# A decoder layer on one core: the input and its first block of weights laid side by side in memory, in six transfers

## The chip, the cores and the metric

The kernel runs on one core of one Trainium2 chip, as a single launch. The metric is device time in microseconds (us). TensorE (PE) multiplies matrices, VectorE (DVE) and ScalarE (ACT) work element by element, GpSimd (POOL) and SyncE (SP) mostly start transfers, and 16 DMA engines carry them between the chip's memory (DRAM) and the core's own buffers of 128 partitions.

## The reference

One decoder layer over 256 tokens of 1024 features. The input is normalised, multiplied by one wide matrix, passed through four mixers of four heads each, multiplied by an output matrix, normalised, and added to the input:

```
h = rmsnorm(x, pre_norm_g)                      # x: 256 x 1024
proj = h @ w_in                                 # w_in: 1024 x 4104
p_gdn, p_hgrn, p_moba, p_diff = split(proj)     # 1032, 1024, 1024, 1024 columns
y = concat([gdn_branch(p_gdn), hgrn2_branch(p_hgrn), moba_branch(p_moba), diff_branch(p_diff)])
x = x + rmsnorm(y @ w_out, post_norm_g)         # w_out: 1024 x 1024
```

The first mixer (gated delta rule) takes q, k, v from the first 768 columns through a short convolution, forms a 64x64 lower triangular system for each chunk of 64 tokens and head, solves it, and runs a recurrence over the chunks. The second is a gated linear recurrence, the third and the fourth are softmax attentions. Each mixer has a gate of its own.

## The kernel before

**The products.** The host cuts w_in into eight blocks of columns (`W_BLOCKS`): gkq (q and k of the first mixer, 512 wide), gv (its v and gates, 520 wide), mqk and mvz (third mixer), dqk and dvz (fourth), hqf and hiz (second). A block is used in four pieces of 256 rows (two slices k of 128). Each product must hold more precision than one pass gives, so every weight piece `raw` is split into a rounded part `whi` (a copy on ACT) and the rest `wlo` (a subtraction on DVE), and x transposed is split in the same way into `hT_hi` (ACT) and `hT_lo` (DVE). TensorE then adds three products, hi by hi, lo by hi and hi by lo: 24 matmuls of 128x256 to a piece, 96 to a block. There are six `raw` buffers (here raw_96, 99, 102, 105, 111, 112) and four each of `whi` and `wlo`, so a later piece is loaded when an earlier one has been split, and is split when TensorE is through with an earlier one.

**The start.** ACT's queue brings the per-column constants and the first slice of x transposed (`pxt`) into a buffer tagged h_kd. SP's queue brings the rest: gkq in four transfers of 256 KB and two of 512 KB, between them the other seven slices of x (four transfers into buffers tagged prob), then gv in four pieces, with `xs` (x itself, for the norm) after the first, then the constants `cs` and `pr`, then the other weights. A row of such a transfer is 1 to 2 KB long per partition for x, 2 to 4 KB for the weights. The norm's factor is worked out from `xs` beside the products and multiplied in afterwards (`rs`, then `rrow`); the first that needs it on DVE is `t2k<-pj,rrow`.

**The middle.** From there DVE runs the convolution, the triangular systems and their inversion (`g_nb`, `g_y`, `g_d`), whose last two steps are `g_ya` and its transposition `g_xa`. TensorE needs g_xa for `gA<-g_xa,g_ee`, where the first mixer's recurrence starts. Between them DVE also writes the `wlo` of the blocks that TensorE multiplies meanwhile (mqk, dqk, mvz, then hqf). Of a block, the products with wlo may come later than those with whi.

**The order.** No scheduler of the compiler sets it. Every operation is recorded by `record` with a cost, and `Core.plan` simulates the engines with these costs and always takes the ready operation with the highest rank: the longest path to the end, plus `boost` (where the code marks a load or a split as urgent), plus `LEAD` for the part of the kernel it belongs to. `HOLD`, `SWITCH` and `STAY` say how dearly the planner takes a change of ACT's table and of TensorE's tile shape. `emit` (line 392, so nearly every row of the trace has L392; L405 in the changed kernel) then issues the operations in that order. So new costs and new leads move operations on every engine.

Of the kernel before, what the change touches and what calls it, by code (L numbers as in the profile page):

```python
# [16 lines left out]
try:  # L17
# [21 lines left out]
C_DQ, C_DK, C_DV, C_DZ = 3080, 3336, 3592, 3848  # L39


W_BLOCKS = (("gkq", C_GQ, 512), ("gv", C_GV, 520), ("hqf", C_HQ, 512), ("hiz", C_HI, 512),
            ("mqk", C_MQ, 512), ("dqk", C_DQ, 512), ("mvz", C_MV, 512), ("dvz", C_DV, 512))


K_TRI, K_AFT, K_BLK, K_BM, K_I16 = 0, 128, 256, 288, 292
# [45 lines left out]


class Op:
    __slots__ = ("eng", "fn", "args", "kw", "cost", "need", "preds", "succs", "rank", "left", "at", "order", "boost", "groups", "work", "part", "lat", "mode")


class Core:
# [2 lines left out]

    SETS = {AF.Exp: 6, AF.Ln: 6, AF.Silu: 18}
    OUT = ("out", "accum_out", "dst")
    HOLD = 34479
    SWITCH, KEEP, STAY = 95, 1e9, 8733
    LEAD = {'h': 7522, 'g': 6523, 'o': -111940, 'M': 5144, 'x': 39478, 'm': 28417, 'd': 3696, 'D': 2624}
    WINDOW = 4096 / 1.2
    LAT = {"PE": 200, "DVE": 170, "ACT": 170, "POOL": 170, "SP": 2600}

    def __init__(self, ctx, tc):  # L110
        self.tc, self.nc = tc, tc.nc
        nc = tc.nc
# [5 lines left out]
        self.boost, self.part = 0.0, "x"  # L118
        self.phys, self.turn, self.masks = {}, {}, {}
        self.sbuf, self.psum = {}, {}  # L120

# [50 lines left out]
    def record(self, eng, fn, cost, writes, reads, args, kw, need=None):  # L172
        op = Op()
        op.eng, op.fn, op.args, op.kw, op.cost, op.need = eng, fn, args, kw, cost, need
        op.preds, op.succs, op.boost, op.groups, op.work = set(), [], self.boost, (0, 1, 2, 3), 0.0
        op.part, op.lat, op.mode = self.part, self.LAT[eng], (128, 128)
        me = len(self.ops)
        for w, aps in ((False, reads), (True, writes)):
            for ap in aps:
                name = ap.tensor.name  # L180
                if name in self.psum:

                    b = self.psum[name]
# [40 lines left out]
    def mm(self, out, lhsT, rhs, start=True, stop=True, **kw):  # L224
        n, m = self.size(rhs), lhsT.shape[1]
        full = 1.667 if rhs.dtype == F else .417
        cost = max(n * full, m * full) + 2 if rhs.dtype == F else max(n * .446, 107) + 4.5
        self.record("PE", "matmul", cost, [out], [lhsT, rhs], (out,),
                    dict(lhsT=lhsT, rhs=rhs, start=start, stop=stop, **kw))
        p, m = self.rows(out)  # L230
        o = self.ops[-1]
        if 2 < m < 128:
            o.groups = tuple(range(p // 32, (p + m + 31) // 32))
        k = self.rows(rhs)[1]
# [60 lines left out]
    def plan(self, noise=None):  # L295
# [22 lines left out]
        cols, mode, work = [0.0] * 4, (128, 128), {}  # L318
        while events:
            t = events[0][0]  # L320
            while events and events[0][0] <= t:
# [3 lines left out]
            for e, q in ready.items():  # L325
# [32 lines left out]
                if e == "PE":  # L358
# [9 lines left out]
                    end = o.at + cost * slow  # L368
                    for g in o.groups:
                        cols[g] = end  # L370
                    free[e] = end if len(o.groups) == 4 else o.at + 7 * slow
                heapq.heappush(events, (free[e], 1, -1))
                for s in o.succs:
                    n = ops[s]
# [17 lines left out]
            getattr(self.engines[o.eng], o.fn)(*o.args, **o.kw)  # L392


def build(tc, x, pxt, w_in, w_out, cst, prow, out, dbg=None):
    with ExitStack() as ctx:
        _build(Core(ctx, tc), x, pxt, w_in, w_out, cst, prow, out, dbg)


def bc(ap, n):  # L400
# [2 lines left out]
    return ap.unsqueeze(len(s)).to_broadcast(s + [n])  # L403


def _build(c, x, pxt, w_in, w_out, cst, prow, out, dbg):
# [6 lines left out]
    px = c.tile("px", [128, 512], tag="h_kd")  # L413
    pc = c.tile("pc", [128, P_END])
    pr = c.tile("pr", [128, R_POST])

    xr = [c.tile("xr", [128, 2, T], tag=f"prob_{i}") for i in range(4)]
# [22 lines left out]

    def piece(key, k):

        if (key, k) not in HI:
            t = c.tmp("raw", [128, 2, 520], bufs=6)
            w, o = BLOCKS[key], BLOCK_AT[key] + k * 128 * BLOCKS[key]
            part = bass.AP(tensor=w_in.tensor, offset=w_in.offset + o, ap=[[2 * w, 128], [w, 2], [1, w]])
            lead = sum(1 for q in HI if q[0] != "o")
            first = lead < 4
            if first:
                for i in range(2):  # L450
                    c.boost = turn(k + i) - 0.05 * BOOST
                    c.dma(t[:, i, :w], part[:, i])
            else:
                c.boost = turn(k) - 0.05 * BOOST if lead < 8 else turn(8) if lead < 10 else 0.0
                c.dma(t[:, :, :w], part)
            split([(key, k), (key, k + 1)], t[:, :, :w], first, not lead)
        return HI[key, k], LO[key, k]

    def split(keys, raw, apart=False, first=False):

        w = raw.shape[2]
        c.boost = BOOST
        hi = c.tmp("whi", [128, 2, 520], bufs=4, dt=FR)[:, :, :w]
        lo = c.tmp("wlo", [128, 2, 520], bufs=4, dt=FR)[:, :, :w]
        for i in ([slice(0, 1), slice(1, 2)] if apart else [slice(0, 2)]):
            if first and i.start == 0:
                c.copy(hi[:, i], raw[:, i])
            else:
                act(hi[:, i], raw[:, i], AF.Copy)
            c.tt(lo[:, i], raw[:, i], hi[:, i].bitcast(F), OP.subtract)  # L470
# [24 lines left out]
    for k in range(8):  # L495
        c.boost = BOOST + 500.0
        g = px[:, P_PRE + k:P_PRE + k + 1]
        xk = xr[k // 2][:, k % 2] if k else px[:, P_END:P_END + T]
# [729 lines left out]
def _arrays(inputs):  # L1228
# [9 lines left out]
    xt = a["x"].reshape(T, 8, 128).transpose(2, 1, 0).reshape(128, 8 * T)  # L1238
    blocks = [a["w_in"][0][:, c0:c0 + w].reshape(4, 2, 128, w).transpose(0, 2, 1, 3).reshape(-1) for _, c0, w in W_BLOCKS]
    return {"x": a["x"].reshape(T, D), "pxt": np.ascontiguousarray(np.concatenate([pcol, xt], axis=1)),  # L1240
            "w_in": np.concatenate(blocks)[None], "w_out": a["w_out"][0], "cst": _shape_constants(),
            "prow": np.ascontiguousarray(prow)}


# [15 lines left out]
```

## Time and profile before

| | us |
|---|---|
| median of 3 runs (167.80 to 168.16) | 168.05 |
| the profiled execution | 168.47 |
| its span | 166.7 |
| TensorE busy in the span | 157.4 |
| VectorE busy | 133.0 |
| ScalarE busy | 108.3 |
| GpSimd busy | 18.8 |

The clock granted to TensorE was 0.997 of full speed, the upper of its two levels (2.4 GHz), in the mean. TensorE counts as busy for 94% of the span, but its matmuls overlap: one of 128x256 is shown with 0.28 us and the next starts some 0.12 us after it, so the distance between starts tells more than the busy time. A row of a timeline gives the start, the duration, the engine, the operation with what it writes and reads, and in brackets how long the engine had been idle before and who released it. Rows with x2 are several instructions that follow each other.

### The profile page before, as it was taken

What the parts mean: (1) busy time and instruction counts of PE and PEld (TensorE: products, weight loads), DVE (VectorE), ACT (ScalarE), POOL (GpSimd) and SP (SyncE); (2) the same over time, 40 slices, a digit from 0 to 9 for tenths busy, and PEclk for the clock granted to TensorE, in tenths of its full rate; (3) what the DMA queues carried; (4) which work ended last, traced back from release to release, by engine and by line L of the source; (5) the groups of instructions that cost most, each with busy time, mean ns of one, the idle gap of its engine ahead of it and who ended that gap; (6) DMA issues with size and microseconds to landing.
All of it is one profiled execution on the core that took longest, in us unless ns stands there. A gap on an engine that the chain in (4) does not pass through costs nothing.

```text
span 166.7 us, 3622 instructions
## 1 busy us (share of the span) xinstructions
PE 157.4 (94%) x1351; PEld 138.1 (83%) x1351; DVE 133.0 (80%) x356; ACT 108.3 (65%) x214; POOL 18.8 (11%) x39
## 2 busy tenths in 40 slices
PE   7899999999999999997999999999999999999950
PEld 5699999999886989996899968877778798987850
DVE  0779589998999999996898598699699977428472
ACT  3678459999169986550059987999599353650450
POOL 8600000000001000077065200000000000000000
PEclk9999999999999999999999999999999999999998
DMA  5999998177870005936359886148603400000033
GB/s 165 317 413 412 361 397 322 29 241 225 275 261 0 0 4 168 309 91 128 127 153 243 179 264 240 34 145 286 236 0 129 126 0 4 0 0 0 0 126 126
DMA packets 14256, 27.24 MB, mean 163 GB/s; under 512 B 1440, under 2 KB 2720, under 8 KB 14240
## 3 DMA queue, kind: packets, MB, share of 16 engines
q1 hardware_dynamic: 12944, 25.31, 44.8%
q0 software_dynamic: 1152, 1.57, 4.8%
q8 instruction: 10, 0.16, 0.4%
q10 hardware_dynamic: 144, 0.15, 0.3%
q14 instruction: 6, 0.05, 0.1%
HBM read 24.14 MB, written 1.05 MB: 151 GB/s over the span
## 4 chain that ended last, share of the span: by engine, by line
PE 60%; DVE 23%; DMA 9%; issue 3%; ACT 2%; SPq 1%; DVEq 0%; ACTq 0%
PE pj L392 39%; DMA raw<-in_w_in_dram 9%; PE gA L392 7%; PE gB L392 6%; PE wB L392 4%; PE wA L392 4%; DVE g_nb L392 4%; DVE wlo L392 3%; DVE g_ee L392 2%; DVE y L392 1%; DVE g_kdec L392 1%; DVE g_y L392 1%; DVE prob L392 1%; ACT whi L392 1%; DVE g_vb L392 1%
## 5 line engine op out<-in xcount | busy, mean ns | idle before, releaser
L392 DVE TENSOR_TENSOR wlo<-raw,whi 128x1024 fp32r<-128x1024 f32 (+2 forms) x42 | 48.3, 1173 | 12.4 <-ACT whi L392 7.6
L392 ACT ACTIVATE whi<-raw 128x1024 fp32r<-128x1024 f32 (+2 forms) x41 | 41.0, 1023 | 6.8 <-DMA raw<-in_w_in_dram 3.6
L392 PE MATMUL pj<-hT_hi,whi 128*128 128x256 f32 x144 | 36.8, 289 | 0.7 <-ACT hT_hi L392 0.7
L392 PE MATMUL pj<-hT_lo,whi 128*128 128x256 f32 x144 | 36.5, 288 | 0.0
L392 PE MATMUL pj<-hT_hi,wlo 128*128 128x256 f32 x144 | 28.7, 284 | 0.0
L392 PEld LDWEIGHTS pj<-hT_hi,whi 128*128 128x128 f32 x144 | 26.6, 190 | 1.9 <-ACT hT_hi L392 1.4
L392 PEld LDWEIGHTS pj<-hT_lo,whi 128*128 128x128 f32 x144 | 26.3, 188 | 0.3 <-issue 0.2
L392 PE MATMUL pj<-whi,hT_lo 128*128 128x512 f32 (+2 forms) x80 | 26.3, 348 | 0.0
L392 PEld LDWEIGHTS pj<-hT_hi,wlo 128*128 128x128 f32 x144 | 22.0, 189 | 0.4 <-issue 0.2
L392 PE MATMUL pj<-whi,hT_hi 128*128 128x512 f32 (+2 forms) x64 | 21.2, 344 | 0.0
L392 PE MATMUL pj<-wlo,hT_hi 128*128 128x512 f32 (+2 forms) x64 | 19.9, 353 | 0.2 <-DVE wlo L392 0.2
L392 PEld LDWEIGHTS pj<-whi,hT_lo 128*128 128x128 f32 x80 | 15.0, 188 | 1.6
L390 ACT ACT_TABLE_LOAD x11 | 14.1, 1283 | 1.4 <-PEq L1250 1.2
L392 PEld LDWEIGHTS pj<-whi,hT_hi 128*128 128x128 f32 x64 | 12.0, 189 | 1.2
L392 PEld LDWEIGHTS pj<-wlo,hT_hi 128*128 128x128 f32 x64 | 11.1, 189 | 1.6 <-DVE wlo L392 0.4
L392 ACT ACTIVATE prob<-prob,mx 128x128 f32<-128x128 f32 (+1 forms) x24 | 10.6, 445 | 0.1
L392 DVE CUSTOM_DVE_ANT_0 prob<-wB,cs 128x128 f32<-128x128 f32 (+1 forms) x24 | 8.0, 354 | 1.7 <-PE wB L392 1.6
L392 PE MATMUL pj<-whi,d_st 128*128 128x512 f32 (+1 forms) x32 | 9.1, 371 | 0.0
L392 POOL MEMSET vexp<- 128x1024 f32 x3 | 2.8, 948 | 46.6 <-PE wB L392 46.6
L392 POOL DMA_DIRECT2D d_st<-d_ks x12 | 6.2, 514 | 16.8 <-ACT d_ks L392 16.8
L392 ACT ACTIVATE t2k<-pj 128x512 f32<-128x512 f32 (+1 forms) x4 | 2.2, 544 | 8.9 <-PE pj L392 8.9
L392 ACT ACTIVATE g_za<-gA 32x256 f32<-32x256 f32 x2 | 0.8, 376 | 9.9 <-PE gA L392 9.8
(271 smaller groups left out, 301.0 us busy)
## 6 DMA issues: line engine op xcount, KB each, us to landing
raw<-in_w_in_dram SPq DMA_DIRECT2D x26, 512.0 KB, 5.5
raw<-in_w_out_dram SPq DMA_DIRECT2D x8, 512.0 KB, 4.8
raw<-in_w_in_dram SPq DMA_DIRECT2D x4, 520.0 KB, 9.9
raw<-in_w_in_dram SPq DMA_DIRECT2D x4, 256.0 KB, 4.1
xs<-in_x_dram SPq DMA_DIRECT2D x2, 512.0 KB, 8.4
prob<-in_pxt_dram SPq DMA_DIRECT2D x3, 256.0 KB, 6.1
d_st<-d_ks POOLq DMA_DIRECT2D x12, 64.0 KB, 3.1
d_st<-qk4k POOLq DMA_DIRECT2D x12, 64.0 KB, 3.5
```

The lines of the kernel that those rows point to most:

```text
L390: nc.scalar.add_instruction(mybir.InstLoadActFuncSet(name=nc.get_next_instruction_name(), act_func_set_id=cur, ins=[], outs=[]))
L392: getattr(self.engines[o.eng], o.fn)(*o.args, **o.kw)
```

## The change

The block gkq leaves `W_BLOCKS`. The host writes, slice by slice, the 256 columns of x transposed and the 512 columns of gkq next to each other into one tensor `xw`, so that one partition's row of a slice is 768 floats, 3 KB. `XW_PARTS` cuts it into six transfers, all on SP's queue: the constants with slice 0 (803 floats per partition), slices 1, 2 and 3 (768 each), and slices 4-5 and 6-7 (1536 each, 6 KB). They land in six buffers whose first use comes later in the kernel: g_eb, sall, g_ee, d_ks, m_pt, d_pt. The rest of the start reads x and gkq from there. Since gkq takes no `raw` buffer any more, two of the six are free when gv is loaded, and the first two pieces of mqk are loaded ahead of `cs` and `pr`.

The planner changes too: a matmul that fills only a part of the 128x128 array costs 20 more, is counted by rows and columns of the array (16 fields instead of 4), and leaves the engine after 12 instead of 7; HOLD, STAY and every LEAD have new values. (The slot `tie` is there but nothing sets it.) That moves operations all through the program. The number of matmuls in the program is the same, 1119.

```diff
-W_BLOCKS = (("gkq", C_GQ, 512), ("gv", C_GV, 520), ("hqf", C_HQ, 512), ("hiz", C_HI, 512),
+W_BLOCKS = (("gv", C_GV, 520), ("hqf", C_HQ, 512), ("hiz", C_HI, 512),
             ("mqk", C_MQ, 512), ("dqk", C_DQ, 512), ("mvz", C_MV, 512), ("dvz", C_DV, 512))
+XW_PARTS = (("g_eb", 1024, 35 + 768), ("sall", 1024, 768), ("g_ee", 1024, 768), ("d_ks", 1024, 768),
+            ("m_pt", 1536, 1536), ("d_pt", 1536, 1536))
...
-    HOLD = 34479
-    SWITCH, KEEP, STAY = 95, 1e9, 8733
-    LEAD = {'h': 7522, 'g': 6523, 'o': -111940, 'M': 5144, 'x': 39478, 'm': 28417, 'd': 3696, 'D': 2624}
+    HOLD = 322786
+    SWITCH, KEEP, STAY = 95, 1e9, 14930
+    LEAD = {'h': -554, 'g': 9086, 'o': -128620, 'M': 8482, 'x': 10483, 'm': 29315, 'd': 11178, 'D': -15230}
...
+        a, b = (range(x // 32, (x + n) // 32) if n < 96 else range(4) for x, n in ((q, o.mode[0]), (p, o.mode[1])))
+        o.groups = tuple(4 * i + j for i in a for j in b)
+        if len(o.groups) < 16:
+            o.cost += 20
...
-                    free[e] = end if len(o.groups) == 4 else o.at + 7 * slow
+                    free[e] = end if len(o.groups) == 16 else o.at + 12 * slow
...
-    c.boost = turn(0)
-    c.dma(px[:, 0:P_END + T], pxt[:, 0:P_END + T], "ACT")
-    for a, b in ((1, 2), (2, 4), (4, 6), (6, 8)):
-        c.boost = turn(a)
-        c.dma(xr[a // 2][:, a % 2:a % 2 + b - a],
-              pxt[:, P_END + a * T:P_END + b * T].rearrange("p (k t) -> p k t", t=T))
+    XW, o = [], 0
+    for k, (tag, n, w) in enumerate(XW_PARTS):
+        t = c.tile("xw", [128, n], tag=tag)
+        for i in range(w // 768):
+            a = w % 768 + 768 * i
+            XW.append((t, a))
+        c.boost = turn(len(XW) - 1)
+        c.dma(t[:, 0:w], bass.AP(tensor=xw.tensor, offset=xw.offset + o, ap=[[w, 128], [1, w]]))
+        o += 128 * w
+    px = XW[0][0]
...
-        if (key, k) not in HI:
+        if key == "gkq" and (key, k) not in HI:
+            t, a = XW[k]
+            if XW[k + 1 - 2 * (k % 2)][0] is t:
+                split([(key, k), (key, k + 1)], t[:, a:a + 1536].rearrange("p (i c) -> p i c", i=2)[:, :, T:])
+            else:
+                split([(key, k)], t[:, None, a + T:a + 768], not k)
+        elif (key, k) not in HI:
```

What SP issues first, before. prob and h_kd are buffers of x, raw those of weights (ACT issues h_kd's):

```order
L392 DMA raw_96<-in_w_in_dram 128x512 x2
L392 DMA prob_68<-in_pxt_dram 128x256
L392 DMA raw_99<-in_w_in_dram 128x512
L392 DMA prob_69<-in_pxt_dram 128x512
L392 DMA raw_99<-in_w_in_dram 128x512
L392 DMA raw_102<-in_w_in_dram 128x2x512
L392 DMA prob_70<-in_pxt_dram 128x512
L392 DMA raw_105<-in_w_in_dram 128x2x512
L392 DMA prob_71<-in_pxt_dram 128x512
L392 DMA raw_111<-in_w_in_dram 128x1040
L392 DMA xs<-in_x_dram 128x1024 x2
```

The same place after:

```order
L405 DMA g_eb<-in_xw_dram 128x803
L405 DMA sall<-in_xw_dram 128x768
L405 DMA g_ee<-in_xw_dram 128x768
L405 DMA d_ks<-in_xw_dram 128x768
L405 DMA m_pt<-in_xw_dram 128x1536
L405 DMA d_pt<-in_xw_dram 128x1536
L405 DMA raw_107<-in_w_in_dram 128x1040
L405 DMA xs<-in_x_dram 128x1024 x2
```

Six transfers stand where eleven stood (ten of SP and one of ACT), and gv and xs follow in the same order as before.

On DVE, the last operations ahead of g_xa, before:

```order
L392 TENSOR_TENSOR g_nb_134<-g_nb_134,g_y_133 128x8x2
L392 TENSOR_TENSOR g_y_133<-g_y_133,g_nb_134 128x8x2
L392 TENSOR_TENSOR g_nb_135<-g_nb_135,g_y_133 128x8
L392 TENSOR_TENSOR g_y_133<-g_y_133,g_nb_135 128x8
L392 TENSOR_TENSOR g_ya<-g_y_133,cs 128x512
L392 STREAM_TRANSPOSE g_xa<-g_ya 128x512
L392 TENSOR_TENSOR g_za<-gA_83,cs 128x512
L392 TENSOR_TENSOR wlo_98<-raw_102,whi_97 128x2x512
```

And after; the four wlo are the block hqf's:

```order
L405 TENSOR_TENSOR d_ks<-d_ks 128x512
L405 TENSOR_TENSOR g_nb_131<-g_nb_131,g_y_129 128x8
L405 TENSOR_TENSOR wlo_101<-raw_143,whi_100 128x2x512
L405 TENSOR_TENSOR wlo_103<-raw_144,whi_102 128x2x512
L405 TENSOR_TENSOR wlo_97<-raw_107,whi_96 128x2x512
L405 TENSOR_TENSOR wlo_99<-raw_108,whi_98 128x2x512
L405 TENSOR_TENSOR g_y_129<-g_y_129,g_nb_131 128x8
L405 TENSOR_TENSOR qk4k<-qk4k 128x512
L405 TENSOR_TENSOR g_ya<-g_y_129,cs 128x512
L405 TENSOR_TENSOR gz_moba<-pj_95,rrow 128x512
L405 STREAM_TRANSPOSE g_xa<-g_ya 128x512
L405 TENSOR_TENSOR g_za<-gA_84,cs 128x512
```

Four wlo of hqf and gz_moba, which stood behind g_xa and g_za, now stand ahead of g_xa.

On TensorE, around the matmuls that need g_xa, before (wlo_98 is a piece of mvz):

```order
L392 MATMUL pj_110<-hT_hi,whi_106 128x256
L392 MATMUL pj_110<-hT_lo,whi_106 128x256
L392 MATMUL pj_94<-wlo_98,hT_hi 128x256 x2
L392 MATMUL pj_95<-hT_hi,wlo_98 128x256 x2
L392 MATMUL pj_94<-wlo_98,hT_hi 128x256
L392 MATMUL gA_83<-g_xa,g_ee 64x64 x16
L392 MATMUL pj_94<-wlo_98,hT_hi 128x256
L392 MATMUL pj_95<-hT_hi,wlo_98 128x256 x2
```

And after (wlo_97 and wlo_99 are pieces of hqf; all of mvz's stand further ahead):

```order
L405 MATMUL pj_106<-hT_hi,whi_96 128x256
L405 MATMUL pj_106<-hT_hi,wlo_97 128x256
L405 MATMUL pj_106<-hT_hi,whi_98 128x256
L405 MATMUL pj_106<-hT_lo,whi_98 128x256
L405 MATMUL pj_106<-hT_hi,wlo_99 128x256
L405 MATMUL gA_84<-g_xa,g_ee 64x64 x16
L405 MATMUL pj_106<-hT_hi,whi_98 128x256
```

Of the dense 256-wide matmuls 34 more stand ahead of gA in the changed program (40 new, 6 gone behind), all products with wlo of mvz and hqf.

## Rows read from the trace of the kernel before

**Rows 1.** Page, part 1: busy time, share of the span, instructions:
```profile
PE 157.4 (94%) x1351; PEld 138.1 (83%) x1351; DVE 133.0 (80%) x356; ACT 108.3 (65%) x214; POOL 18.8 (11%) x39
```
**Rows 2.** Stretches: length, busy and count per engine, granted clock, DMA share, GB/s:
```profile
4.77:17.73 12.96, 12.31 (x96) 12.02 (x97) 10.56 (x19) 9.19 (x16) 2.04 (x4) 1.00 1.02 388
17.73:30.39 12.66, 12.51 (x105) 12.22 (x104) 10.27 (x25) 9.26 (x16) 0.00 (x0) 1.00 0.89 327
24.12:77.14 53.02, 51.72 (x432) 48.29 (x431) 51.33 (x173) 38.94 (x77) 6.02 (x12) 1.00 0.52 163
77.19:160.80 83.61, 83.55 (x759) 69.60 (x759) 64.13 (x150) 53.65 (x109) 6.72 (x14) 1.00 0.39 116
160.80:166.70 5.90, 0.00 (x1) 0.00 (x0) 2.00 (x5) 0.97 (x4) 0.00 (x0) 0.93 0.29 104
```
**Rows 3.** Chain of waits, from its start to g_xa's user: start, us, what:
```profile
9.81 10.57 DMA raw<-in_w_in_dram
20.46 1.08 ACT whi L392
21.57 1.25 DVE wlo L392
...
75.70 0.70 DVE g_ya L392
76.43 0.72 DVE g_xa L392
77.19 1.15 PE gA L392 x32
```
**Rows 4.** Timeline of PE at the start:
```profile
4.77 0.80 PE L392 MATMUL pj<-hT_hi,whi 128*128 128x256 f32 x2
...
8.17 0.50 PE L392 MATMUL pj<-hT_hi,whi 128*128 128x256 f32 x2 [0.65 <-ACT hT_hi L392]
```
**Rows 5.** The first 21 us in stretches of 2 us, columns as in rows 2:
```profile
2.08:4.17 2.09, 2.09 (x12) 1.47 (x11) 0.15 (x1) 0.44 (x1) 2.03 (x3) 1.00 0.94 311
4.17:6.25 2.08, 2.06 (x11) 1.50 (x9) 2.08 (x6) 1.55 (x3) 2.02 (x5) 1.00 0.93 261
6.25:8.33 2.08, 1.43 (x11) 1.22 (x10) 1.14 (x4) 1.35 (x3) 0.56 (x1) 1.00 1.03 374
8.33:10.42 2.09, 2.09 (x19) 2.09 (x20) 1.43 (x3) 1.38 (x3) 0.00 (x0) 1.00 1.05 407
...
14.58:16.67 2.09, 2.09 (x19) 2.09 (x19) 1.94 (x3) 1.47 (x3) 0.00 (x0) 1.00 1.03 413
...
18.75:20.83 2.08, 2.08 (x20) 2.00 (x19) 1.45 (x2) 0.58 (x3) 0.00 (x0) 1.00 0.97 313
```
**Rows 6.** Timeline of ACT and DVE where gv's last pieces and the norm's factor arrive:
```profile
20.46 1.08 ACT L392 ACTIVATE whi<-raw 128x1040 fp32r<-128x1040 f32 x1 [1.50 <-DMA raw<-in_w_in_dram]
...
24.12 1.28 DVE L392 TENSOR_TENSOR t2k<-pj,rrow 128x512 f32<-128x512 f32 x2
```
**Rows 7.** Timeline of DVE in the middle: two wlo, and the longest wait:
```profile
35.60 2.36 DVE L392 TENSOR_TENSOR wlo<-raw,whi 128x1024 fp32r<-128x1024 f32 x2
...
39.10 1.22 DVE L392 TENSOR_TENSOR wlo<-raw,whi 128x1024 fp32r<-128x1024 f32 x1 [0.61 <-ACT whi L392]
```
**Rows 8.** All operations on gz_moba: duration min/median/max in ns, first and last start:
```profile
L392 DVE TENSOR_TENSOR gz_moba<-pj,rrow x1: 687/687/687, 88.5 to 88.5; 128x512 f32<-128x512 f32 x1
```
**Rows 9.** Timeline of PE ahead of the matmuls that need g_xa:
```profile
74.81 0.29 PE L392 MATMUL pj<-hT_lo,whi 128*128 128x256 f32 x1
...
75.40 0.41 PE L392 MATMUL pj<-wlo,hT_hi 128*128 128x256 f32 x2
75.64 0.40 PE L392 MATMUL pj<-hT_hi,wlo 128*128 128x256 f32 x2
75.88 0.28 PE L392 MATMUL pj<-wlo,hT_hi 128*128 128x256 f32 x1
77.19 1.15 PE L392 MATMUL gA<-g_xa,g_ee 64*64 64x64 f32 x32 [1.03 <-DVE g_xa L392]
```
**Rows 10.** Timeline of PE where it leaves the full tile and comes back:
```profile
89.98 0.28 PE L392 MATMUL pj<-hT_lo,whi 128*128 128x256 f32 x1
90.19 0.45 PE L392 MATMUL gB<-g_vn,g_kdec 64*64 64x64 f32 x8
90.47 0.40 PE L392 MATMUL gA<-g_vn,g_ee 64*64 64x64 f32 x8
90.80 0.39 PE L392 MATMUL pj<-hT_hi,whi 128*128 128x256 f32 x1
91.03 0.28 PE L392 MATMUL pj<-hT_lo,whi 128*128 128x256 f32 x1
```

More of the change, by code (lines that the diff above doesn't have):

```diff
@@ L94 @@
 class Op:
-    __slots__ = ("eng", "fn", "args", "kw", "cost", "need", "preds", "succs", "rank", "left", "at", "order", "boost", "groups", "work", "part", "lat", "mode")
+    __slots__ = ("eng", "fn", "args", "kw", "cost", "need", "preds", "succs", "rank", "left", "at", "order", "boost", "groups", "work", "part", "lat", "mode", "tie")
 class Core:
@@ L117, in __init__ @@
         self.ops = []
-        self.boost, self.part = 0.0, "x"
+        self.boost, self.part, self.tie = 0.0, "x", None
         self.phys, self.turn, self.masks = {}, {}, {}
@@ L174, in record @@
         op.eng, op.fn, op.args, op.kw, op.cost, op.need = eng, fn, args, kw, cost, need
-        op.preds, op.succs, op.boost, op.groups, op.work = set(), [], self.boost, (0, 1, 2, 3), 0.0
-        op.part, op.lat, op.mode = self.part, self.LAT[eng], (128, 128)
+        op.preds, op.succs, op.boost, op.groups, op.work = set(), [], self.boost, range(16), 0.0
+        op.part, op.lat, op.mode, op.tie = self.part, self.LAT[eng], (128, 128), self.tie
         me = len(self.ops)
@@ L229, in mm @@
                     dict(lhsT=lhsT, rhs=rhs, start=start, stop=stop, **kw))
[L230 to L234, printed above, removed]
+        (p, m), (q, k), o = self.rows(out), self.rows(rhs), self.ops[-1]
         o.mode = (32 if k <= 32 else 64 if k <= 64 else 128 if k > 96 else 96, 32 if m <= 32 else 64 if m <= 64 else 128)
+        a, b = (range(x // 32, (x + n) // 32) if n < 96 else range(4) for x, n in ((q, o.mode[0]), (p, o.mode[1])))
+        o.groups = tuple(4 * i + j for i in a for j in b)
+        if len(o.groups) < 16:
+            o.cost += 20
         o.work = n * full * k / 128
@@ L311, in plan @@
                 o.rank += noise[i]
+        ties = {}
+        for o in ops:
+            if o.tie is not None:
+                ties.setdefault(o.tie, []).append(o)
+        for tied in ties.values():
+            top = max(o.rank for o in tied)
+            for o in tied:
+                o.rank = top
         ready = {e: [] for e in self.engines}
@@ L317, in plan @@
         order, cur = [], 6
-        cols, mode, work = [0.0] * 4, (128, 128), {}
+        cols, mode, work = [0.0] * 16, (128, 128), {}
         while events:
@@ L392, in emit, with build @@
             getattr(self.engines[o.eng], o.fn)(*o.args, **o.kw)
-def build(tc, x, pxt, w_in, w_out, cst, prow, out, dbg=None):
+def build(tc, x, xw, w_in, w_out, cst, prow, out, dbg=None):
     with ExitStack() as ctx:
-        _build(Core(ctx, tc), x, pxt, w_in, w_out, cst, prow, out, dbg)
+        _build(Core(ctx, tc), x, xw, w_in, w_out, cst, prow, out, dbg)
 def bc(ap, n):
@@ L403, in bc, with _build @@
     return ap.unsqueeze(len(s)).to_broadcast(s + [n])
-def _build(c, x, pxt, w_in, w_out, cst, prow, out, dbg):
+def _build(c, x, xw, w_in, w_out, cst, prow, out, dbg):
     mm, tr, act = c.mm, c.tr, c.act
@@ L412, in _build @@
     xs = c.tile("xs", [128, 2, D])
-    px = c.tile("px", [128, 512], tag="h_kd")
     pc = c.tile("pc", [128, P_END])
     pr = c.tile("pr", [128, R_POST])
-    xr = [c.tile("xr", [128, 2, T], tag=f"prob_{i}") for i in range(4)]
     turn = lambda k: BOOST * (4.0 - 0.2 * k)
-    c.boost = turn(0)
-    c.dma(px[:, 0:P_END + T], pxt[:, 0:P_END + T], "ACT")
-    for a, b in ((1, 2), (2, 4), (4, 6), (6, 8)):
-        c.boost = turn(a)
-        c.dma(xr[a // 2][:, a % 2:a % 2 + b - a],
-              pxt[:, P_END + a * T:P_END + b * T].rearrange("p (k t) -> p k t", t=T))
+    XW, o = [], 0
[8 more added lines that the diff above has]
+    px = XW[0][0]
     for j in range(2):
@@ L446, in piece, with split @@
             part = bass.AP(tensor=w_in.tensor, offset=w_in.offset + o, ap=[[2 * w, 128], [w, 2], [1, w]])
[L447 to L456, printed above, removed]
+            c.boost = turn(8) if len(HI) < 10 else 0.0
+            c.dma(t[:, :, :w], part)
+            split([(key, k), (key, k + 1)], t[:, :, :w])
         return HI[key, k], LO[key, k]
-    def split(keys, raw, apart=False, first=False):
-        w = raw.shape[2]
+    def split(keys, raw, first=False):
+        n, w = raw.shape[1:]
         c.boost = BOOST
[L463 to L470, printed above, removed]
+        hi = c.tmp("whi", [128, 2, 520], bufs=4, dt=FR)[:, 0:n, :w]
+        lo = c.tmp("wlo", [128, 2, 520], bufs=4, dt=FR)[:, 0:n, :w]
+        if first:
+            c.copy(hi, raw)
+        else:
+            act(hi, raw, AF.Copy)
+        c.tt(lo, raw, hi.bitcast(F), OP.subtract)
         for i, key in enumerate(keys):
@@ L497, in _build @@
         g = px[:, P_PRE + k:P_PRE + k + 1]
-        xk = xr[k // 2][:, k % 2] if k else px[:, P_END:P_END + T]
+        t, a = XW[k]
+        xk = t[:, a:a + T]
         act(hh_t[:, k], xk, AF.Copy, scale=g)
@@ L1237, in _arrays @@
                                                       "diff_lq2", "diff_lk2", "post_norm_g")])[None]
[L1238 to L1242, printed above, removed]
+    xt = a["x"].reshape(T, 8, 128).transpose(1, 2, 0)
+    wi = a["w_in"][0]
+    first = [np.concatenate([xt[k], wi[k * 128:(k + 1) * 128, 0:512]], axis=1) for k in range(8)]
+    parts, k = [], 0
+    for _, _, w in XW_PARTS:
+        n = w // 768
+        parts.append(np.concatenate(([pcol] if w % 768 else []) + first[k:k + n], axis=1).reshape(-1))
+        k += n
+    blocks = [wi[:, c0:c0 + w].reshape(4, 2, 128, w).transpose(0, 2, 1, 3).reshape(-1) for _, c0, w in W_BLOCKS]
+    return {"x": a["x"].reshape(T, D), "xw": np.concatenate(parts)[None], "w_in": np.concatenate(blocks)[None],
+            "w_out": a["w_out"][0], "cst": _shape_constants(), "prow": np.ascontiguousarray(prow)}
 def kernel(**inputs):
```

## The prediction

> **What bounds the kernel now.** I read the page's first part, then stretches, then the chain of waits, then the timelines at the places that the chain names. The first part shows TensorE busy 94% of the span and DVE 80% [rows 1], which by itself would say that only TensorE counts. The stretches show three regimes [rows 2]. Up to 30.39 us TensorE multiplies gkq and gv. From 24.12, where DVE can first use the norm's factor, to 77.14, where it has written g_xa, DVE is busy 51.33 of 53.02 us. From 77.19 to 160.80 TensorE is busy 83.55 of 83.61 us, and a tail of 5.90 us follows. The chain of waits confirms the seams [rows 3]: it starts with a load of weights that takes 10.57 us and lands at 20.38, goes over ACT and DVE, and enters TensorE for good at 77.19 through g_ya and g_xa. TensorE has run out of other work there: its last dense matmul starts at 75.88, the next could start 0.12 us later, and g_xa lets it go on at 77.19 [rows 9]. So it stalls 1.19 us. Hence two things can move the end: when DVE's stretch starts, with how much lies in it, and how much TensorE still has to do behind g_xa.
>
> **The start.** The change makes rows of 3 and 6 KB out of rows of 1 to 4 KB, and one queue's six transfers out of eleven on two queues. The bytes are the same, about 3.2 MB for x and gkq, and what is queued behind them up to gv's last piece is the same too. So the arrival of gv is what the rate of the DMA engines makes of it. The rate is 407 to 413 GB/s from 8.33 to 16.67 us, with rows of 2 to 4 KB, but 311, 261 and 374 GB/s in the three stretches before it, although the engines' share is 0.94, 0.93 and 1.03: packets are slow there, and engines not idle [rows 5]. The lower end of the gain is that these slow stretches have nothing to do with the layout and come again. Then 3.2 MB at 413 in place of 407 GB/s is worth 0.1 us. The upper end is that they go: 311 x 2.09 + 261 x 2.08 + 374 x 2.08 = 1,971 KB would take 4.77 us at 413 GB/s in place of 6.25, 1.48 us less. A second slow stretch, 313 GB/s at 18.75 [rows 5], is where cs and pr with their short rows are in flight beside the end of gv; after, two pieces of mqk with 4 KB rows stand in their place. At 413 GB/s it would be 0.50 us shorter. So gv's end can come 0.1 to 2.0 us earlier. The part of the low rate in the first stretch that is only the start-up of the transfers stays. I take **1.2 us**, a little over the middle, because the lowest rate lies where the 1 KB rows of x run between the weights.
>
> The Trainium skill ("HBM Reference", section Specifications (TRN2)) states about 358 GB/s as a core's share of the memory, and that a core alone measures well above it, about 425 GB/s, bounded by its 16 DMA engines. By 358 nothing could come earlier; the trace has 413 GB/s [rows 5] and refutes that end for this core alone. By 425 the steady stretches could gain 3%, an estimate of 0.5 us over 18 us.
>
> TensorE has room to take an earlier arrival. Its 96 matmuls of gkq take 12.96 us and those of gv 12.66 [rows 2], while a dense one of 256 columns starts every 0.118 us (five from 74.81 to 75.40 [rows 9]), which makes 11.3 us for 96. The 1.7 and 1.3 us between are waits for pieces, most of the first in one hole before 8.17 us, when x's third slice was late [rows 4]. On DVE the same 1.2 us shows as an earlier `t2k<-pj,rrow`, now at 24.12: gv's third piece is split at 20.46, after a wait of 1.50 us for its load, and everything up to t2k follows [rows 6].
>
> The lost parallel queue costs nothing, I take it: the first transfer carries on one queue what landed by two before, in both cases some 400 KB ahead of TensorE's first matmul at 4.77 [rows 4]. Bounds: 0.4 us later to 0.2 us earlier, since DVE's load of the first x would have to wait for all of it; that is hidden behind the hole before 8.17.
>
> **DVE's stretch.** In the changed order four more wlo of 1024 elements (hqf's) and gz_moba stand between t2k and g_xa. Two such wlo in a row take 2.36 us, the second starts some 1.14 us after the first (2.36 less 1.22) [rows 7]. So 4 x 1.14 = 4.56 us; gz_moba lasts 0.69 and overlaps its neighbour a little [rows 8], 0.6; and two small copies, 0.15. Sum **+5.3 us** (5.0 to 5.5). The stretch has 53.02 - 51.33 = 1.7 us of idle time [rows 2], of which 0.61 is one wait of wlo for ACT's whi [rows 7]; with mqk's first two pieces loaded earlier this one may go. I take **-0.3** (0 to -0.6). So g_xa comes at 77.14 + 5.3 - 0.3 - 1.2 = 80.9.
>
> **TensorE around it.** Ahead of gA stand 34 more dense matmuls, all with wlo of mvz and hqf: 34 x 0.118 = **4.0 us**. It would be there at 76.0 + 4.0 less what its own start gained, 1.2: 78.8. So it waits 2.1 us in place of 1.19, and g_xa still sets the time. Behind g_xa it has 4.0 us less to do. DVE too has that much less to do behind g_xa, so it is not late for what follows. hqf's wlo need TensorE to be through with mvz's wlo in the same buffers, and its hqf matmuls need those wlo: small waits both ways, all ahead of a wait that is there anyway.
>
> **Tile shapes.** Each time TensorE leaves the full tile and comes back something is lost: from 89.98 to 91.03 lie two dense matmuls (0.24 us) and 16 small ones, which by the 32 in 1.15 us [rows 9] cost 0.57, and 1.05 us have passed [rows 10]. So 0.24 us are lost per excursion. Counted through the program, the shape changes 61 times before and 55 times after, three excursions less: 0.7 us. I take **-0.6** (0 to -1.0, since kf's matmuls in halves may overlap better or worse).
>
> **New waits** behind g_xa, from a new order on all engines: TensorE is almost never idle there now [rows 2], so any wait that the order brings is a loss. The trace of before cannot show one. The nearest rows are the waits that exist, 0.61 and 1.03 us [rows 7, 9]; none is likely to be gained, so 0 to +1.0, and I take **+0.2**, near nothing.
>
> Sum: -1.2 + 5.3 - 0.3 - 4.0 - 0.6 + 0.2 = -0.6 us. The profiled execution (168.47 us with a span of 166.7) lies 0.4 us over the median; the differences carry over. 168.05 - 0.6 = 167.45, rounded to **167.4 us**.
>
> **The rivals.** *The slow start comes again* (slower). If the slow packets of the first 8 us belong to the start and not to the rows, gv comes 0.1 to 0.3 us earlier and no more. Then DVE's longer stretch decides: -0.3 + 5.3 - 0.3 - 4.0 - 0.3 + 0.3 = +0.7, 168.75 us; with no gain at the tiles +1.0. The point from which it decides is an arrival of gv less than 0.6 us earlier, that is `t2k<-pj,rrow` after 23.5 us. For it speaks that in the steady stretch rows of 2 KB run as fast as rows of 4 KB; against it, that the lowest rate coincides with 1 KB rows.
>
> *The whole gain* (much faster). Both slow stretches go, gv ends 2.0 us earlier, and the tile shapes give their 0.7: -2.0 + 5.3 - 0.3 - 4.0 - 0.7 + 0.1 = -1.6, 166.45 us, and with the second half of DVE's idle time 165.9. Against it: ACT and DVE have their own work in the start, and DVE is busy 10.56 of 12.96 us during gkq [rows 2].
>
> *The layout changes no arrival* and the order no end: the extra wlo fall in what would have been DVE's idle time, TensorE fills its wait, 168.05. The chain through g_ya and g_xa [rows 3] speaks against so exact a balance.
>
> **How the numbers follow.** Forecast 0.5 (its own range 166.8 to 168.2, most of it faster), the slow start 0.28 (168.4 to 169.1), the whole gain 0.17 (165.8 to 166.6), no change 0.05. The range that leaves out 2 in 10, half on either side: 165.9 to 168.9. What this kernel's measurement can tell from no change is about 0.2%, 0.34 us. Faster: 0.38 of the forecast's 0.5 and 0.17, so 0.55; the same: 0.10 of the forecast, 0.05 of no change and 0.02 of the slow start, 0.17; slower: 0.02 and 0.26, 0.28.
>
> **What would show it.** Right: rates near 400 GB/s between 4 and 8 us, no hole of 0.65 us in TensorE's start, t2k at about 22.9, DVE busy without a break up to g_xa at about 81, a stall of TensorE of some 2 us before gA, and from gA to the last matmul about 79.2 us in place of 83.6. Wrong: t2k at 24, or waits of TensorE behind g_xa; or if TensorE arrives at gA after g_xa is there, which would mean that the early matmuls and not DVE set the end, and that the four wlo were free.

## The result and the profile after

The changed kernel takes 173.44 us (171.46 to 173.89) against 168.11 us of the kernel before (167.80 to 168.41): a ratio of 1.0268, interval 1.0232 to 1.0305. It is 2.7% slower, 4.5 us by that ratio and 5.3 us by the medians, where 0.6 us less was forecast and 168.9 us was the end of the range. The profiled execution took 173.89 us, the longest of the four.

Two rows of the page of the changed kernel: TensorE's busy share and its granted clock in 40 slices of the span (172.2 us), in tenths.

```profile
PE   7999999999999999997299999999999999999960
PEclk9999999999999999999957999999999999999998
```

Four stretches of the changed kernel, columns as in rows 2, to which they answer:

```profile
4.62:30.05 25.43, 25.20 (x200) 24.84 (x199) 20.26 (x38) 18.07 (x31) 2.23 (x4) 1.00 0.94 358
22.93:80.66 57.73, 56.34 (x473) 52.88 (x471) 55.99 (x181) 41.73 (x82) 6.05 (x12) 1.00 0.53 171
80.71:166.31 85.60, 82.15 (x725) 67.83 (x725) 58.58 (x145) 50.59 (x105) 6.70 (x14) 0.96 0.33 101
166.31:172.20 5.89, 0.00 (x0) 0.00 (x0) 2.00 (x5) 0.97 (x4) 0.00 (x0) 0.89 0.29 101
```

gkq and gv are through TensorE at 30.05 us, 0.34 earlier than before. DVE's stretch begins at 22.93, 1.19 earlier, and ends at 80.66, 3.52 later. Both were nearly forecast (22.9 and 80.9). The last row, the tail, is as before. The loss lies in the third row: from gA to TensorE's last matmul it takes 85.60 us, where 83.61 was before and 79.2 forecast. In the slices TensorE has one of 0.2 busy and, just behind it, two with a granted clock of 0.5 and 0.7.

The timeline of TensorE in the changed kernel shows the place. It answers to rows 9.

```profile
79.16 0.28 PE L405 MATMUL pj<-hT_hi,wlo 128*128 128x256 f32 x1
80.71 1.15 PE L405 MATMUL gA<-g_xa,g_ee 64*64 64x64 f32 x32 [1.27 <-DVE g_xa L405]
...
82.48 0.28 PE L405 MATMUL pj<-hT_hi,wlo 128*128 128x256 f32 x1
85.86 0.66 PE L405 MATMUL wB<-d_st 128*128 128x128 f32 x2 [3.10 <-DMA d_st<-qk4k]
...
88.94 0.41 PE L405 MATMUL pj<-hT_hi,whi 128*128 128x256 f32 x1
89.16 0.41 PE L405 MATMUL pj<-hT_lo,whi 128*128 128x256 f32 x1
...
92.89 0.33 PE L405 MATMUL wB<-d_st 128*128 128x128 f32 x1
```

TensorE could go on at 82.60 and goes on at 85.86: 3.26 us in which it waits for a transfer, d_st<-qk4k. From there a dense matmul starts every 0.22 us (88.94, 89.16) and not every 0.12. The stretches of 2 us around it, the granted clock third from the end:

```profile
82.00:84.00 2.00, 0.76 (x6) 0.56 (x5) 0.60 (x1) 0.00 (x0) 0.00 (x0) 1.00 1.14 330
84.00:86.00 2.00, 0.14 (x1) 0.17 (x2) 0.00 (x0) 0.00 (x0) 0.00 (x0) 0.91 0.73 125
86.00:88.00 2.00, 2.00 (x31) 1.88 (x32) 0.67 (x5) 0.70 (x4) 0.00 (x0) 0.50 0.00 0
88.00:90.00 2.00, 2.00 (x15) 1.88 (x14) 1.48 (x5) 0.17 (x2) 0.56 (x2) 0.50 0.00 0
90.00:92.00 2.00, 2.00 (x10) 1.66 (x9) 1.53 (x5) 0.42 (x1) 2.00 (x5) 0.50 0.49 109
92.00:94.00 2.00, 2.00 (x40) 1.79 (x40) 0.60 (x5) 1.93 (x5) 0.36 (x1) 0.89 0.43 96
```

The clock falls to the lower of its two levels (0.50 of 2.4 GHz) at the end of the wait and comes back in the last row. From 86.00 to 92.44 it is 0.50 throughout, so TensorE works some 6.6 us at half speed. What they cost shows where the same operations run at 1.00. From the first wB to the next one of its form they take 7.03 us here (85.86 to 92.89) and 4.17 us in the kernel with the wait filled, below (86.02 to 90.19), so 2.9 us less. So the wait costs twice, 3.26 + 2.9 = 6.1 us, and 85.60 - 6.1 = 79.5 is near the 79.2 that the prediction had for this stretch.

Why the transfer is late is in the chain of waits of the changed kernel (start, us, what), which enters TensorE here and no longer at gA, as it did in rows 3:

```profile
74.45 3.70 DVE wlo L405 x4
78.15 0.09 DVE g_y L405
78.24 0.61 DVE qk4k L405
78.85 0.28 issue
79.12 0.48 POOL d_st L405
79.61 6.23 DMA d_st<-qk4k
85.83 0.02 issue
85.86 0.66 PE wB L405 x2
```

The rounding of qk4k stands on DVE behind hqf's four wlo, and GpSimd moves qk4k into d_st for the first scores of the differential attention. So those moves start at 79.1, and the one that TensorE needs takes 6.23 us to land.

### The profile page after: what moved, and what is told of

Its sections match the earlier page's. It is cut to its first block, busy times and chain, and to the rows that moved or that the text cites. A ratio compares the mean times of both kernels' runs of the same rounds, so it can differ in the third digit from the quotient of the medians.

```text
span 172.2 us, 3614 instructions
## 1 busy us (share of the span) xinstructions
PE 160.0 (93%) x1351; PEld 140.9 (82%) x1351; DVE 131.9 (77%) x356; ACT 107.6 (62%) x214; POOL 19.0 (11%) x39
## 4 chain that ended last, share of the span: by engine, by line
PE 75%; DMA 7%; DVE 7%; ACT 5%; issue 2%; SPq 0%; DVEq 0%; POOL 0%; ACTq 0%
PE pj L405 51%; PE gB L405 8%; PE gA L405 6%; PE wB L405 5%; PE wA L405 5%; DMA d_st<-qk4k 4%; DMA g_ee<-in_xw_dram 3%; DVE wlo L405 3%; ACT whi L405 2%; DVE y L405 2%; ACT L403 1%; DVE b4k L405 1%; ACT prob L405 1%; SPq L405 0%; ACT d_pt L405 0%
## 5 line engine op out<-in xcount | busy, mean ns | idle before, releaser
L405 DVE TENSOR_TENSOR wlo<-raw,whi 128x1024 fp32r<-128x1024 f32 (+1 forms) x36 | 42.6, 1221 | 5.5 <-PE gA L405 3.3
L405 ACT ACTIVATE whi<-raw 128x1024 fp32r<-128x1024 f32 (+1 forms) x36 | 37.2, 1056 | 11.1 <-PE pj L405 5.2
L405 PE MATMUL pj<-hT_hi,whi 128*128 128x256 f32 x144 | 38.8, 300 | 0.0
L405 PE MATMUL pj<-hT_lo,whi 128*128 128x256 f32 x144 | 37.8, 292 | 0.0
L405 PE MATMUL pj<-hT_hi,wlo 128*128 128x256 f32 x144 | 31.6, 288 | 0.4 <-DVE wlo L405 0.4
L405 PEld LDWEIGHTS pj<-hT_hi,whi 128*128 128x128 f32 x144 | 27.5, 198 | 0.9 <-ACT g_au L405 0.4
L405 PEld LDWEIGHTS pj<-hT_lo,whi 128*128 128x128 f32 x144 | 27.6, 198 | 0.0
L405 PEld LDWEIGHTS pj<-hT_hi,wlo 128*128 128x128 f32 x144 | 23.2, 191 | 1.0 <-DVE wlo L405 0.8
L405 PE MATMUL pj<-wlo,hT_hi 128*128 128x512 f32 (+2 forms) x64 | 19.4, 348 | 0.0
L405 POOL DMA_DIRECT2D d_st<-qk4k x12 | 6.0, 501 | 13.3 <-PE wB L405 10.3
```

## The experiments

The kernel without the loads computes something else; the others compute the same. Where an order is put in by hand, the planner still runs, and its list of operations is then edited or replaced by a list that is written out.

**The layout alone.** The changed kernel's loads and buffers, with every later operation in the order that the kernel before has on each engine.

```diff
         order, _ = self.plan()
+        order = list(ORDER_BEFORE)
```

> The new layout (six transfers of x and gkq side by side) with every later operation in the order of the kernel before, on all engines. Theory A, the layout is a gain and the new order the loss: in the changed kernel DVE's first use of the norm's factor came at 22.93 us in place of 24.12, so 1.2 us earlier, and with the old order that goes on to g_xa (about 75.9) and to the end: 168.1 - 1.2 = 166.9 us, not over 167.3. Rival B, the layout is the loss (six long transfers on one queue disturb what comes later): 170 us or more, and the d_st moves land late here too.

Measured: 168.81 against 168.61 us, ratio 0.9995 (0.9968 to 1.0022). Neither: the layout does no harm, and gains nothing in this order. DVE's t2k starts at 23.65 in place of 24.12, yet g_xa starts at 76.47 (76.43 before). DVE's lead goes in a wait for ACT that the kernel before doesn't have (0.59 us, for v_diff, at 33.30 us). TensorE gains nothing in the start either, and ACT's timeline of this kernel shows one reason:

```profile
7.33 0.63 ACT L486 ACTIVATE whi<-g_ee 128x512 fp32r<-128x512 f32 x1 [1.15 <-DMA g_ee<-in_xw_dram]
7.87 0.49 ACT L486 ACTIVATE hT_hi<-g_ee,g_eb 128x256 fp32r<-128x256 f32 x1
```

The third slice of x and its weights now land together, at 7.3 us, and in the old order ACT takes the weights first. TensorE's hole, which ended at 8.17 before [rows 4], ends at 8.41 here. It is through with gv at 30.47 us (30.39 before).

**The order alone.** Loads and layout of the kernel before, every later operation in the changed kernel's order, by a list in the same way.

> The other half: loads and layout of the kernel before, every later operation in the order of the changed kernel. Theory A: the same wait of TensorE for the moved qk4k and the same fall of its clock as in the changed kernel, with a start that is 1.2 us later: 173.4 + 1.2 = 174.6 us. Rival B: 168 to 169 us, no such wait.

Measured: 172.78 us (170.86 to 174.00), ratio 1.0254 (1.0192 to 1.0316). The four wlo are ahead of qk4k (73.71 to 78.34), and qk4k's late move starts at 79.31. So the new order is what costs, with the old layout as with the new one. The further 1.2 us of the old layout did not show. Nor did the fall of the clock, in the one execution that was profiled, the shortest of the four (170.86 us). TensorE could go on at 82.80 and waits 2.54 us for the same transfer, and the clock (third from the end of the last row) stays at 1.00:

```profile
82.68 0.28 PE L474 MATMUL pj<-hT_hi,wlo 128*128 128x256 f32 x1
85.34 0.41 PE L474 MATMUL wB<-d_st 128*128 128x128 f32 x2 [2.39 <-DMA d_st<-qk4k]
...
86.00:88.00 2.00, 2.00 (x40) 1.93 (x35) 1.58 (x9) 0.88 (x4) 0.44 (x1) 1.00 0.00 0
```

So the wait comes with the order and the lower clock doesn't always come with the wait. This execution is 2.3 us over the kernel before (168.61) and 1.7 over the same kernel with qk4k first (169.13, below), about what the wait alone costs. The other three took 172.60 to 174.00 us at a lower mean clock (0.981 to 0.986, here 0.990), but no trace of theirs shows where.

**qk4k first.** The changed kernel with one operation moved on DVE: 914 is the rounding of qk4k, 1154 the first wlo of hqf.

```diff
+MOVES = ((914, 1154),)
...
         order, _ = self.plan()
+        for a, b in MOVES:
+            order.remove(a)
+            order.insert(order.index(b), a)
```

> The changed kernel with one operation moved: DVE's rounding of qk4k (128x512) stands ahead of the four wlo of hqf in place of behind them. Theory A, its moves to d_st start 4.6 us too late because of the four wlo: they are issued at about 74.5 to 76, land before TensorE comes to its first matmul with d_st at 82.6, the wait of 3.1 us and the half clock behind it (about 3.3 us) are gone: 173.4 - 6.4 = 167.0 us. Rival C, the moves are slow because four loads of 512 KB are in flight with them, whenever they start: they still land at 84 or later and most of the loss stays, 171 us or more.

Measured: 168.32 us, ratio 0.9962 (0.9936 to 0.9989); 167.0 was too low by 1.3, but the whole loss is gone. Of the 1.3 the profiled executions explain 0.7: the half clock cost 2.9 and not 3.3 us, and gA starts at 81.04 in place of 80.71. The late move starts at 76.4 in place of 79.1. The moves are slow here too, as rival C says: the three of qk4k issued from 76.2 to 79 us land after 5.2 us in the median, beside the same loads. But they are early enough. In the timeline TensorE passes the place without a wait:

```profile
82.81 0.28 PE L416 MATMUL pj<-hT_hi,wlo 128*128 128x256 f32 x1
82.93 0.34 PE L416 MATMUL wB<-d_st 128*128 128x128 f32 x2
```

The granted clock is 1.00 in each stretch of 2 us from 82 to 88. One operation of 0.6 us in the wrong place thus cost 3% (1.0268 to 0.9962).

**The wait filled.** The changed kernel; 28 dense matmuls run on TensorE ahead of its first one with d_st.

```diff
         for i in order:
             o = ops[i]
+            if i == 923:
+                for _ in range(28):
+                    nc.tensor.matmul(self.phys["wA0"][:, 0:256], lhsT=..., rhs=..., start=True, stop=True)
```

> The changed kernel with 28 dense matmuls of 128x256 put on TensorE, into a bank that nothing uses then, ahead of its first matmul with d_st: 28 x 0.118 = 3.3 us, as long as the wait. They add no delay if the moves land as late as before, and TensorE is not idle. Theory A, the idle time costs twice, once itself and once through the granted clock of 0.50 for the 6.5 us behind it: the clock stays at 1.00 and the time is 173.4 - 3.3 = 170.1 us. Rival D, the clock falls for another reason: 173.4 us and 0.50 again.

Measured: 171.09 us, ratio 1.0133 (1.0085 to 1.0181). The timeline of TensorE in this kernel:

```profile
82.67 3.51 PE L408 MATMUL wA<-hT_hi 128*128 128x256 f32 x28
86.02 0.33 PE L413 MATMUL wB<-d_st 128*128 128x128 f32 x2
...
90.19 0.44 PE L413 MATMUL wB<-d_st 128*128 128x128 f32 x2
```

Its stretch of 2 us behind the wait, the granted clock third from the end:

```profile
86.00:88.00 2.00, 2.00 (x41) 1.86 (x40) 1.20 (x6) 0.87 (x4) 0.00 (x0) 1.00 0.03 8
```

The 28 matmuls hold TensorE until 86.02, as the wait held it until 85.86 (the moves themselves land a little earlier here, 5.8 us after their issue and not 6.5). The clock stays at 1.00, and the time is 1.35% (some 2.3 us) under the changed kernel's. So the loss of 3.1% falls into about 1.7% for the wait (1.0133 to 0.9962) and 1.35% for the clock. The half clock was forecast at 3.3 us and is worth some 2.3 in the medians; 2.9 is its cost in the longest of the changed kernel's executions, and from one execution to the next it need not be the same.

**No loads beside it.** The changed kernel without the four loads of weights that SP starts when the four wlo free their buffers.

```diff
         for i in order:
             o = ops[i]
+            if i in (1287, 1302, 1438, 1450):
+                continue
```

> The changed kernel without the four loads of 512 KB (weights for later blocks) that SP starts at 74 to 80 us, when the four wlo free their buffers; what is computed from them is not the reference's. It tells whether the moves to d_st land late because they start late or because of these loads. Theory A2, both are needed: the moves start at 79.1 as before, land within about 3 us like the first of them, TensorE comes to d_st at 82.6 and goes on at once, the clock stays at 1.00: about 168.4 us. Rival E, the late start alone explains the wait: landing at 84 or later, 171 us or more.

Measured: 167.99 us, ratio 0.996 (0.9941 to 0.9978), though qk4k stands as late as in the changed kernel. The DMA issues of the changed kernel from 78.5 to 87 us: count, KB of one, median us from issue to landing.

```profile
raw<-in_w_in_dram SPq DMA_DIRECT2D x1, 512.0 KB, 8.2
d_st<-qk4k POOLq DMA_DIRECT2D x3, 64.0 KB, 6.3
d_st<-d_ks POOLq DMA_DIRECT2D x2, 64.0 KB, 6.0
```

The same view of the kernel without the loads:

```profile
d_st<-qk4k POOLq DMA_DIRECT2D x6, 64.0 KB, 1.9
d_st<-d_ks POOLq DMA_DIRECT2D x4, 64.0 KB, 2.0
```

A move of 64 KB lands after 6.3 us beside the loads, and after 1.9 us without them. So the late start alone would have cost next to nothing: started at 79.1 and landing 2 us later, qk4k would have been there before 82.6. Nor would the loads alone have cost anything: with qk4k first they slow the moves, and TensorE doesn't wait. It takes both, and both are the work of the four wlo. They hold qk4k back by 4.6 us, and they free four buffers, whereupon 2 MB of weights are on the way just when the small moves start.

**g_xa first.** The changed kernel with DVE's last steps to g_xa, and qk4k, ahead of the four wlo, by a written list. On DVE: g_y, qk4k, g_ya, g_xa, wlo, g_za, gz_moba, wlo, wlo, wlo. On TensorE: of hqf's first 48 products 14 with whi, then gA, the other 18 with whi, 8 with wlo, then gB and wB, then the last 8 with wlo.

> The changed kernel with DVE's last steps to g_xa, and qk4k with them, ahead of the four wlo of hqf; TensorE takes 14 of hqf's products with whi, then gA, then the other products with whi, and those with wlo behind them. Theory A: g_xa at about 76.1 in place of 80.7 and no wait of TensorE ahead of gA (1.4 us before); against qk4k moved alone (168.3) another -1.4: 166.9 us. Rival F, DVE's work is only moved, and the wlo that come 2 us later stop TensorE in turn: 168.3 us or more.

Measured: 166.72 against 168.53 us, ratio 0.9874 (0.9849 to 0.99). It beats both kernels, by 1.3% and by 3.8%. TensorE's timeline of this kernel, where gA waited 1.4 us in the changed one:

```profile
75.56 0.28 PE L486 MATMUL pj<-hT_lo,whi 128*128 128x256 f32 x1
75.77 1.15 PE L486 MATMUL gA<-g_xa,g_ee 64*64 64x64 f32 x32
76.85 0.39 PE L486 MATMUL pj<-hT_hi,whi 128*128 128x256 f32 x1
...
82.27 0.50 PE L486 MATMUL wB<-d_st 128*128 128x256 f32 x2 [0.60 <-DVE mx L486]
```

DVE's order is a list of what others wait for, not only a sum of work: the same four wlo, ending 3.5 us later (81.66 in place of 78.15), cost one wait of 0.60 us, for mx, which DVE works out behind them. Several operations moved at once here; what each is worth was not told apart.

**GpSimd's writes later.** qk4k first, and GpSimd's seven early MEMSETs behind a small transfer that waits until some 15 us.

```diff
+        late = [61, 796, 62, 63, 65, 64, 66]
+        order = [i for i in order if i not in late]
+        at = order.index(48) + 1
+        order[at:at] = late
...
+            if i == 61:
+                nc.gpsimd.dma_start(self.tile("late", [128, 8]), self.phys["hT_lo"][0][:, 2040:2048])
```

> qk4k moved ahead as in qk4k_first, and seven MEMSETs of GpSimd (into vexp, d_st, reset, ath), which run from 1 to 6.9 us, started only after 15 us, behind a small transfer that waits for the last hT_lo. It tells whether the low rate at 4 to 6 us (261 to 310 GB/s, once 192, in old and new layout alike) comes from these writes. Theory G, it does: above 390 GB/s from 4 to 8 us, the pause of TensorE before 8.5 us shrinks by 0.5 to 0.8 us, 167.7 us. Rival H, the low rate belongs to the start whatever GpSimd does: rates below 320 again, 168.3 us.

Measured: 168.66 us, ratio 1.0003 (0.9983 to 1.0023). The rate from 4.17 to 6.25 us is 272 GB/s, as low as ever, so these writes are not its cause. The kernel is 0.4% slower than qk4k first. One of the MEMSETs now makes TensorE wait at 21.7 us (0.44 us, on reset), a wait that the edit brought along; but TensorE is through with gv only 0.1 us later (30.12, 30.02), so that this wait is the reason isn't shown.

**The old layout in the two better orders.** The kernel before with the changed order, once with qk4k first and once with g_xa first.

> The loads and the layout of the kernel before, the order of the changed kernel, and qk4k moved ahead as in qk4k_first; against that run only the layout differs. Theory I, TensorE's first 30 us do not follow the arrival of gv, so the layout is worth nothing there: 168.3 us, within 0.3 of qk4k_first. Rival J, the earlier arrival that the layout brings is worth something once the wait for d_st is gone: 0.6 us or more slower than qk4k_first, 168.9 us or more.

> The loads and the layout of the kernel before, with the order of gxa_first; against gxa_first (0.987 of the kernel before) only the layout differs. Theory I, the layout is worth nothing once the order is given: 0.987 again. Theory K, in the new order TensorE's first products follow the first transfers more closely, and there the layout is worth what the other pair showed (0.7%): 0.994.

Measured: 169.13 us, ratio 1.0034 (1.0018 to 1.005), and 167.75 us, ratio 0.9941 (0.9916 to 0.9966). Against the same orders with the new layout (0.9962 and 0.9874) the old one is 0.7% slower both times, 1.2 us; the first pair's rival and the second's theory K hold. So the layout is a gain of 0.7% in the new order, and of nothing in the old one or behind the wait for d_st. In the profiled runs TensorE is through with gv at 29.84 to 30.12 us in the six kernels with new layout and new order, and at 29.94, 30.44 and 30.99 us in the three with old layout and new order. That is where the 0.7% may come from. It isn't shown: there is one profile of each kernel, and 29.94 with the old layout is as early as the new one.

**Two queues.** g_xa first, with the first of the six transfers issued by ACT's queue.

```diff
-        c.dma(t[:, 0:w], bass.AP(tensor=xw.tensor, offset=xw.offset + o, ap=[[w, 128], [1, w]]))
+        c.dma(t[:, 0:w], bass.AP(tensor=xw.tensor, offset=xw.offset + o, ap=[[w, 128], [1, w]]), "SP" if k else "ACT")
```

> gxa_first with the first of the six transfers issued by ACT's queue, the other five by SP's, so that those start 0.4 us earlier. Theory L, the transfers share the same engines and their rate sets the arrivals: no difference beyond 0.3%, 0.987 of the kernel before, first matmul at 4.6 us. Rival M, issuing on one queue costs: slices 1 to 3 come 0.4 us earlier and the time is 0.3 to 0.4 us less, 0.985.

Measured: 167.53 us, ratio 0.9947 (0.9919 to 0.9976): 0.7% slower than on one queue, against both expectations. Its runs lie near 167.1 and near 168.3 us (166.74 to 168.66). ACT's timeline of this kernel:

```profile
5.10 0.51 ACT L486 ACTIVATE hT_hi<-g_eb 128x256 fp32r<-128x256 f32 x1 [2.59 <-DMA g_eb<-in_xw_dram]
5.51 0.49 ACT L486 ACTIVATE hT_hi<-sall,g_eb 128x256 fp32r<-128x256 f32 x1
5.91 0.61 ACT L486 ACTIVATE whi<-sall 128x512 fp32r<-128x512 f32 x1
6.43 0.49 ACT L486 ACTIVATE hT_hi<-g_ee,g_eb 128x256 fp32r<-128x256 f32 x1
```

The first transfer is issued at 0.80 us in both kernels. It lands 4.3 us later, at 5.10, where it took 2.9 on one queue and landed at 3.77, and the next ones are there as soon as it is. TensorE's first matmul is at 6.10 in place of 4.62. It catches up in part, since the holes behind it go; gv ends at 30.18 (29.84). Where the rest of the 0.7%, 1.2 us, comes from isn't shown. The Trainium skill ("DMA: Bandwidth & Descriptors", section Issuing engines are not separate DMA queues) says that transfers of several engines run on the same 16 DMA engines and interleave; the trace agrees, 3.77 against 5.10 us. What interleaves is late together, and here the first transfer is the one that all wait for. So in this order, that the six stand on one queue is worth as much as the layout.

## Why the prediction was wrong

**The step that failed** is the term "new waits behind g_xa", 0 to +1.0 us, taken as +0.2. It was 6.1 us in the profiled run (3.26 of waiting, 2.9 of half clock) and about 3% by the ratios (1.0268 to 0.9962). It was priced by the waits that exist [rows 7, 9], as if a new one were of their kind, instead of following what was moved. The rows of the order ahead of the prediction show qk4k behind the four wlo; the prediction counted these as 5.3 us ahead of g_xa and did not ask who waits for qk4k. That is GpSimd's moves and then TensorE, which has the matmuls with d_st ahead of everything else. With the wlo's own price, 4 x 1.14 us [rows 7], qk4k would have been seen to leave DVE near 79. The second half, that the wlo free buffers and so start loads that slow these moves from 1.9 to 6.3 us, was not looked for. The third, the clock, was not in the sum at all.

**The start** came out and was worth less. t2k was forecast at 22.9 and came at 22.93, which is in part luck: with the same layout and the new order it starts between 22.88 and 23.87 in the other five kernels, one execution of each. And the step "TensorE has room to take an earlier arrival" was wrong. Of the 1.3 us in gv only 0.3 were a wait (a hole before 22.86 us); the stretch holds 105 matmuls and not 96 [rows 2], many of them 264 columns wide. The 1.7 us in gkq were waits for the first slices, and those came no earlier (275 GB/s from 4.17 to 6.25 us, 261 before [rows 5]): gv's first product starts at 18.12, at 17.73 before. TensorE ended gv 0.34 us earlier, not 1.2. And DVE gave the rest back, in one wait that was not there before:

```profile
22.93 1.28 DVE L405 TENSOR_TENSOR t2k<-pj,rrow 128x512 f32<-128x512 f32 x2
...
30.09 0.69 DVE L405 TENSOR_TENSOR t2k<-wA,rrow 128x512 f32<-128x512 f32 x1 [1.01 <-PE wA L405]
```

DVE waits 1.01 us for the results of gv. Where t2k starts late there is no such wait, and this second t2k starts at the same time (30.05 with qk4k first, whose first t2k starts at 23.87). So an engine that is busy 51.33 of 53.02 us [rows 2] is not bound by itself alone: work that starts earlier runs into the engine that feeds it.

**The lost parallel queue** was right as forecast and understated: first matmul at 4.62 (4.77 before), and two queues for the new transfers cost 0.7% in the one order in which they were tried.

**DVE's stretch** held in size. Its busy time grew by 4.66 us (51.33 to 55.99), forecast 5.3 less 0.3 of idle time; g_xa ended at 80.66, forecast 80.9. **TensorE around it** held too: it could go on at 79.28 (78.8 forecast) and waited 1.43 us (2.1 forecast). **Tile shapes** can't be told apart from the rest. From gA to the last matmul 79.5 us remain without the wait and its clock, and 79.74 with qk4k first (81.04 to 160.78), where 79.2 was forecast. Moving 4.0 us of matmuls ahead of gA thus did what was said.

**The rivals.** None was this. The slow start did come again (275 GB/s), but t2k came early all the same, so the point from which that rival was to decide, t2k after 23.5 us, was the wrong one. With qk4k first t2k starts at 23.87 and that kernel is the faster one. The forecast of -0.6 us is near what the changed kernel does with qk4k first (0.9962, -0.64 us; -0.3 by the medians 168.32 and 168.61), but not by the same terms: the start gave less. That is luck.

## What to carry to other kernels

When a planner moves operations, follow each operation that others on another engine wait for, to its last reader, and not only the sum of work ahead of one known bound. Four long operations put ahead of a short one delay all that hangs on the short one, and what they set free starts at the same time as what they delayed. A wait of TensorE can cost more than its length: here 3.3 us of it brought 2.9 us more through the lower clock behind it, though a wait of 2.5 us in another execution brought nothing more.

## What the runs showed of the hardware

- A transfer of 64 KB from buffer to buffer, issued by GpSimd, landed after 1.9 us with nothing beside it and after 6.3 us beside four loads of 512 KB.
- A wait of 3.3 us on TensorE was followed by some 6.6 us at a granted clock of 0.50, which cost 2.9 us; matmuls that fill the wait kept it at 1.00 and were worth 1.35%. Behind a wait of 2.5 us, in the profiled execution of the order alone, it stayed at 1.00.
- The first of six transfers, issued at 0.80 us, landed at 3.77 us when all were on one queue and at 5.10 us when it alone was on another.
- The low rate of the DMA engines at 4 to 6 us (192 to 310 GB/s in eleven kernels, old and new layout) doesn't come from the length of the rows, nor from GpSimd's writes. It was 418 GB/s in the one kernel with the first of the six on ACT's queue. A second queue alone is not the reason, since the old layout has its first slice of x on ACT's queue too. The cause stays open.
